# Four steps of a two-block network kernel resume a fixed time after their chain of small operations

## The chip, the cores and the metric

The kernel runs on one core of one Trainium2 chip. The metric is device time in microseconds (us) of one execution; lower is better. Of the core's engines, PE (TensorE) does the matrix products, DVE (VectorE) and ACT (ScalarE) work on tiles in SBUF and PSUM, POOL (GpSimd) does small vector work, and SP (SyncE) issues nearly all the transfers. Each engine takes its own instructions in the order in which the program wrote them, and waits at an instruction whose operands another engine has not finished.

## The reference

An activation x of 256 tokens by 1024 features goes through two blocks of two layers each, all in 32-bit floats.

```python
def rms_norm(x, g):
    y = x * rsqrt(mean(x * x, axis=-1) + EPS)
    return y * g

# block 1, each layer
x = x + 0.5 * swiglu(rms_norm(x, norm_ffn1[l]), w_gate, w_up, w_down)       # 1024 -> 2816 -> 1024
x = x + hybrid_mixer(rms_norm(x, norm_mix[l]), w_in[l], ..., w_out[l])      # two kinds of attention
x = x + 0.5 * swiglu(rms_norm(x, norm_ffn2[l]), ...)
# block 2, each layer
p = rmsnorm(x, norm1_g[l]) @ w_in[l]
y_rw  = rwkv7_branch(...)       # a recurrence over the tokens, 8 heads of 64
y_ret = retention_branch(...)
y_sg  = sgu_branch(...)
x = x + sum(gates * einsum('bsgc,gcd->bsgd', [y_rw, y_ret, y_sg], w_branch)) @ w_out[l]
x = x + conv_ffn(rmsnorm(x, norm2_g[l]), ...)
```

Two parts of the recurrence's branch matter here. Its keys are divided by their norms, `kk = kk / max(sqrt(sum(kk*kk)), 1e-12)`, and its result goes through a norm over each head, `(y - mean) * rsqrt(var + RW_GN_EPS) * lnx_g + lnx_b`, plus a bonus, times a gate.

## The kernel before

Tokens are two tiles of 128 (t = 0, 1). The weights, some 340 MB, stream once from memory. Each weight tile of 512 KB (`raw`) is split by ACT into a rounded part `wh` and by DVE into the remainder `wl`; the activations are split in the same way (`xh`, `xl`), and a product is three matmuls (`wh` by `xh`, `wh` by `xl`, `wl` by `xh`). In the profile `cf` and `pj` are PSUM tiles of projections into a layer, `acc` those of projections out of it.

What sets the order is a planner. While the Python code writes the program, the class `Meter` keeps an estimated clock for each engine. The large products are written by plain loops, which call `tick()` after every few matmuls. All the rest (norms, softmax, recurrence, splits of results) is written as generators, held as `Task`s with a rank. A generator that yields stops there, and `step()` says when it may go on: a bare `yield` makes it ready 0.1 us after the latest estimated end of what it has just issued; a list of tiles makes it ready 0.1 us after these; a function makes it wait for a condition. `tick()` runs each task that is ready by the estimated time of PE. So a task's next PE instruction is put behind those of the loop that were written in the meantime, and the real wait is what the estimate had too short. The planner's numbers act only while the program is written; on the chip there is only the order.

The four steps that the change touches:

- `norm()` with `wide` (every phase but block 1's mixers; eight phases, two tiles each): `mean_sq` squares the two halves of x on ACT, and POOL makes `xv` and the power `xr`. Then PE multiplies `xr` by the identity (the matmul `pt<-ident,xr`) to spread the factor along a row, and ACT copies it to `factor`. The projections run on x without the factor; DVE puts it in when it empties their PSUM tiles (`up<-cf,factor`, `up<-pj,factor`).
- `rw_keys()` (both layers of block 2): PE sums the squares of the keys (`pn`), DVE takes a maximum (`n`), POOL raises 128x16 numbers to the power -0.5, and PE spreads them (`pr<-ident,n`).
- `rw_products()`: for each tile and each of 8 heads PE makes masked products in `pM`, DVE copies them under a mask into `mrb` and `lm`, and PE multiplies `lm` by the values (`pX`, `pY`).
- `group_norm()`: four DVE operations on `Y`, then PE transposes it (`pt<-ident,Y`).

Of the kernel before, what the change touches and what calls it, by code (L numbers as in the profile page):

```python
# [222 lines left out]
class Builder:  # L223
# [48 lines left out]
    def step(self, task):  # L272
        self.meter.last = self.meter.t["PE"]
        try:
            y = next(task.gen)
        except StopIteration:
            self.tasks.remove(task)
            return
        if y is None:
            task.ready = self.meter.last + 0.1  # L280
        elif callable(y):
            task.cond = y
        else:
            task.ready = self.meter.of(y) + 0.1
# [246 lines left out]
    def norm(self, t, gi, wide=False, outer=None):  # L531


        nc = self.nc
        F = "p (k f) -> p k f"
        for i in range(2):
            yield from self.have(t, i)
            pt = self.ps("pt")
            for k in range(4):
                c = slice(k * P, (k + 1) * P)  # L540
                nc.tensor.transpose(pt[:, c], self.half(t, i)[:, c], self.ident)
            k = slice(i * 4, i * 4 + 4)
            g = self.gains if outer is None else self.both
            o = gi * KD if outer is None else 0
            g = g[:, o + i * 4:o + i * 4 + 4, None].to_broadcast([P, 4, P])
            xg = self.u("xg").rearrange(F, f=P)
            nc.vector.tensor_tensor(xg, pt.rearrange(F, f=P), g, ALU.mult)
            nc.scalar.copy(self.xh[:, k, t], xg)
            yield [self.xh[:, i * 4, t]]
            nc.vector.tensor_tensor(self.xl[:, k, t], xg, self.xh[:, k, t].bitcast(F32), ALU.subtract)  # L550
            self.ready_xT[t] = i + 1
        yield
        if outer is not None:
            ro = yield from self.row_norm(t, outer)
        r = yield from self.mean_sq(t)
        if outer is not None:
            nc.gpsimd.tensor_tensor(r, r, ro, ALU.mult)
        self.rstd[t] = r
        if wide:
            yield  # L560
            if not self.factor:
                self.factor.append(self.u("factor"))
            pt = self.ps("pt")
            nc.tensor.matmul(pt[:, :P], r.to_broadcast([P, P]), self.ident, start=True, stop=True)
            nc.scalar.copy(self.factor[0][:, t * P:(t + 1) * P], pt[:, :P])
            self.factored.append(t)
# [818 lines left out]
    def heads(self, ap):  # L1385
        return ap.rearrange("p (h d) -> p h d", d=64)

    def wide(self, ap, n=8):
        return ap[:, :, None].to_broadcast([P, n, 64])
# [78 lines left out]
    def rw_keys(self, l, st):  # L1468
# [16 lines left out]
        n = self.small("n2", 16, 2)  # L1485
        nc.vector.tensor_scalar_max(n, pn[:, :16], 1e-24)
        nc.gpsimd.tensor_tensor(n, n, self.mh, ALU.pow)
        yield
        for q in range(2):
            pr = self.ps("pr")  # L1490
            kk.append(self.pairs("kk"))
# [106 lines left out]
    def rw_products(self, l, st):  # L1598

        nc = self.nc  # L1600
        mm = nc.tensor.matmul
        yield lambda: "v" in st
        v = []
        for t in range(NT):
            v.append(self.tokens_on_partitions("vt", st["v"], t))
            yield
        st["vt"] = v
        yield lambda: "KT" in st and "queries" in st
        kr, BT, KT, mrb = (st[n] for n in ("kr", "BT", "KT", "m"))
        mk = self.c("mk3").bitcast(U32)  # L1610
        X, Y = [], []
        for t in range(NT):
            m = mrb[t]
            pX, pY = self.ps("pX", "pq"), self.ps("pY", "pq")
            for h in range(8):
                b, q, e = 64 * (h % 2), h // 4, h // 2 % 2
                pM = self.ps("pM")
                mm(pM[:, 0:P], BT[q][b:b + 64, e, t], kr[q][b:b + 64, e, t, 1], start=True, stop=True)
                mm(pM[:, P:3 * P], KT[q][b:b + 64, e, t], kr[q][b:b + 64, e, t].rearrange("p z f -> p (z f)"), start=True, stop=True)
                lm = st["lm"][h % 4]  # L1620
                nc.vector.copy_predicated(m[:, h], mk[:, 0:P], pM[:, 0:P])
                nc.vector.copy_predicated(lm, mk[:, P:3 * P], pM[:, P:3 * P])
                yield
                c = slice(h * 64, (h + 1) * 64)
                self.narrow(pX[:, c], lm[:, 0:P], v[t][:, c])
                self.narrow(pY[:, c], lm[:, P:2 * P], v[t][:, c])
            X.append(self.u("X"))
            Y.append(self.u("Y"))
            nc.scalar.copy(X[t], pX)
            nc.scalar.copy(Y[t], pY)  # L1630
            yield
        st.update(mrb=mrb, X=X, Y=Y)
# [94 lines left out]
    def group_norm(self, lnx, y, v, bonus, g, done):  # L1727
        nc = self.nc
        tt = nc.vector.tensor_tensor
        heads, wide = self.heads, self.wide  # L1730
        m = self.small("gm", 8)
        nc.vector.tensor_reduce(m, heads(y), AX.X, ALU.add)
        nc.vector.tensor_scalar(m, m, 1.0 / 64, None, ALU.mult)
        tt(heads(y), heads(y), wide(m), ALU.subtract)
        yield
        sq, bv = self.u("gsq"), self.u("gbv")
        nc.scalar.activation(sq, y, AF.Square)
        nc.gpsimd.tensor_tensor(heads(bv), heads(v), wide(bonus), ALU.mult)
        nc.gpsimd.tensor_tensor(bv, bv, lnx[1], ALU.add)
        yield [sq]  # L1740
        s2 = self.small("gs", 8)
        nc.vector.tensor_reduce(s2, heads(sq), AX.X, ALU.add)
        r = self.rstd_of(s2, 64, GN_EPS, 8)
        yield
        tt(heads(y), heads(y), wide(r), ALU.mult)
        tt(y, y, lnx[0], ALU.mult)
        tt(y, y, bv, ALU.add)
        tt(y, y, g, ALU.mult)
        yield
        yield from done(y)  # L1750


# [95 lines left out]
```

## Time and profile before

| what | before |
|---|---|
| median of 3 runs (lowest to highest) | 2075.59 us (2074.72 to 2077.48) |
| the profiled execution's own time | 2073.28 us |
| its span in the trace | 2071.3 us |
| PE busy | 2013.7 us (97%) |
| DVE, ACT, POOL busy | 1394.7, 1043.6, 149.8 us |
| mean rate of the transfers | 166 GB/s |

The span runs from the first to the last instruction of the program; the profiled execution took 2.0 us more than its span, and the median of the runs is 2.3 us above that execution. PE's clock as granted is shown in the profile as a share of full speed: 1.00 is 2.4 GHz and 0.50 is 1.2 GHz.

### The profile page before, as it was taken

Reading aid. Unit: us, or ns where it says so; the run is one execution under the profiler, and the core shown is the slowest. Engines: PE = TensorE matmul, PEld = TensorE weight load, DVE = VectorE, ACT = ScalarE, POOL = GpSimd, SP = SyncE. Lnnn points to the kernel's source line nnn. Section 1 sums busy time; section 2 is a strip of 40 time slices with the busy share of each in tenths; the row PEclk is TensorE's granted clock in tenths of the full one; section 3 lists DMA queues with packets and bytes.
Section 4 is the critical chain, followed back from the end, with each engine's and each line's share of the span. In section 5 each row is a group of like instructions: output and inputs, shape, how many; then the busy total and the mean of one; then the engine's idle time right before and its main releaser. Section 6 shows DMA issues by size and latency. Waiting matters only on the chain. (4 is left out here: it accounts for less than half of the span.)

```text
span 2071.3 us, 33930 instructions
## 1 busy us (share of the span) xinstructions
PE 2013.7 (97%) x13548; PEld 1776.8 (86%) x13548; DVE 1394.7 (67%) x2101; ACT 1043.6 (50%) x1605; POOL 149.8 (7%) x168
## 2 busy tenths in 40 slices
PE   8999999999999999999999999999999999999998
PEld 8998878998999887799887777889988877789997
DVE  6665666664666467666567957669955886667983
ACT  5444675443444366544455434456636444446652
POOL 0000000000000010000021031210001003110000
PEclk9999999999999999999999999999999999999999
DMA  9655623656655562356653434555664453465562
GB/s 315 195 181 152 213 83 113 198 177 194 218 180 185 157 214 92 122 174 193 186 175 114 147 112 136 180 162 177 191 200 134 133 153 98 153 192 176 177 194 97
DMA packets 246733, 343.98 MB, mean 166 GB/s; under 512 B 22064, under 2 KB 182192, under 8 KB 246448
## 3 DMA queue, kind: packets, MB, share of 16 engines
q1 hardware_dynamic: 244224, 340.20, 52.8%
q8 instruction: 106, 1.74, 0.4%
q10 hardware_dynamic: 2352, 1.63, 0.3%
q14 instruction: 51, 0.42, 0.1%
HBM read 339.68 MB, written 2.10 MB: 165 GB/s over the span
## 5 line engine op out<-in xcount | busy, mean ns | idle before, releaser
L191 DVE TENSOR_TENSOR wl<-raw,wh 128x1024 fp32r<-128x1024 f32 (+1 forms) x614 | 750.8, 1236 | 323.9 <-ACT wh L191 323.0
L191 ACT CAST wh<-raw 128x1024 fp32r<-128x1024 f32 (+1 forms) x614 | 639.3, 1046 | 585.9 <-PE cf L191 179.6
L191 PE MATMUL cf<-xh,wh 128*128 128x256 f32 x2112 | 524.7, 285 | 2.4 <-ACT wh L191 2.4
L191 PE MATMUL cf<-xl,wh 128*128 128x256 f32 x2112 | 523.0, 285 | 0.0
L191 PEld LDWEIGHTS cf<-xh,wh 128*128 128x128 f32 x2112 | 409.3, 194 | 3.0 <-ACT wh L191 2.8
L191 PEld LDWEIGHTS cf<-xl,wh 128*128 128x128 f32 x2112 | 409.2, 194 | 0.2
L191 PE MATMUL cf<-xh,wl 128*128 128x256 f32 x2112 | 300.3, 285 | 0.0
L191 PEld LDWEIGHTS cf<-xh,wl 128*128 128x128 f32 x2112 | 275.3, 194 | 0.0
L191 PE MATMUL pj<-wh,xh 128*128 128x512 f32 (+1 forms) x544 | 223.0, 410 | 4.5 <-DVE gate L191 2.0
L191 PE MATMUL pj<-wl,xh 128*128 128x512 f32 (+1 forms) x544 | 211.1, 388 | 0.0
L191 PE MATMUL pj<-wh,xl 128*128 128x512 f32 (+1 forms) x544 | 210.4, 387 | 0.0
L191 PE MATMUL acc<-wh,h 128*128 128x512 f32 x528 | 207.0, 392 | 0.0
L191 PE MATMUL acc<-wh,hl 128*128 128x512 f32 x528 | 205.6, 389 | 0.0
L191 PE MATMUL acc<-wl,h 128*128 128x512 f32 x528 | 205.5, 389 | 0.0
L191 PEld LDWEIGHTS pj<-wh,xh 128*128 128x128 f32 x544 | 102.8, 189 | 36.7 <-issue 9.9
L191 DVE TENSOR_TENSOR up<-cf,factor 128x512 f32<-128x512 f32 x132 | 90.6, 688 | 56.3 <-PE cf L191 56.2
L191 PEld LDWEIGHTS pj<-wh,xl 128*128 128x128 f32 x544 | 102.8, 189 | 21.4
L191 PEld LDWEIGHTS pj<-wl,xh 128*128 128x128 f32 x544 | 103.1, 189 | 16.9 <-DVE wl L191 0.9
L191 PEld LDWEIGHTS acc<-wh,hl 128*128 128x128 f32 x528 | 99.1, 188 | 20.9
L191 PEld LDWEIGHTS acc<-wh,h 128*128 128x128 f32 x528 | 99.2, 188 | 20.0
L191 PEld LDWEIGHTS acc<-wl,h 128*128 128x128 f32 x528 | 99.2, 188 | 19.9
L191 POOL TENSOR_SCALAR xv<-ss 128x1 f32<-128x1 f32 x24 | 20.2, 840 | 1142.6 <-ACT junk L191 1142.6
(314 smaller groups left out, 2489.6 us busy)
## 6 DMA issues: line engine op xcount, KB each, us to landing
raw<-w_in SPq DMA_DIRECT2D x156, 512.0 KB, 4.3
raw<-w_ffn_gate SPq DMA_DIRECT2D x88, 512.0 KB, 4.4
raw<-w_ffn_up SPq DMA_DIRECT2D x88, 512.0 KB, 4.8
raw<-w_ffn_down SPq DMA_DIRECT2D x88, 512.0 KB, 4.2
raw<-ffn_w_up SPq DMA_DIRECT2D x88, 512.0 KB, 4.7
raw<-ffn_w_down SPq DMA_DIRECT2D x44, 512.0 KB, 4.5
raw<-w_out SPq DMA_DIRECT2D x32, 512.0 KB, 3.7
raw<-w_branch SPq DMA_DIRECT2D x24, 512.0 KB, 4.5
```

Of the source, the lines that this page charges most:

```text
L191: return f(*args, **kw)
```

## The change

A generator may now yield a number: `step()` then makes it ready that many microseconds (of the planner's clock) after the latest estimated end, where a bare `yield` said 0.1. Four yields get such a number.

```diff
@@ step()
         if y is None:
             task.ready = self.meter.last + 0.1
+        elif isinstance(y, float):
+            task.ready = self.meter.last + y
         elif callable(y):
             task.cond = y
@@ norm()
         self.rstd[t] = r
         if wide:
-            yield
+            yield 5.0
@@ rw_keys()
         nc.gpsimd.tensor_tensor(n, n, self.mh, ALU.pow)
-        yield
+        yield 3.0
@@ rw_products()
                 nc.vector.copy_predicated(lm, mk[:, P:3 * P], pM[:, P:3 * P])
-                yield
+                yield 0.8
@@ group_norm()
         tt(y, y, g, ALU.mult)
-        yield
+        yield 2.0
         yield from done(y)
```

No instruction is added or taken away by this; the order on each engine changes, since the later steps are written later. Three places show how.

The first is ACT at the start of the second layer of block 1. `junk` are the squares of x, whose two tiles are `x_74` and `x_75`. One piece of the difference, with rows of the later splits left out:

```order
 L191 ACTIVATE junk,ss<-x_74 128x512 x2
 L191 CAST xh<-xg 128x4x128
-L191 CAST wh<-raw 128x1024 x2
-L191 COPY factor<-pt 128x128
-L191 CAST wh<-raw 128x1024
-L191 ACTIVATE junk,ss<-x_75 128x512 x2
...
+L191 CAST wh<-raw 128x1024 x3
+L191 ACTIVATE junk,ss<-x_75 128x512 x2
+L191 CAST wh<-raw 128x1024 x2
+L191 COPY factor<-pt 128x128
+L191 CAST wh<-raw 128x1024
+L191 COPY factor<-pt 128x128
```

Both copies of `factor` stand later, and the squares of the second tile no longer stand behind the first copy. On PE the matmul `pt<-ident,xr` of the first tile stands 48 matmuls of 256 columns later in four of the eight phases, and 44, 44, 45 and 54 later in the others; that of the second tile follows 25 to 85 matmuls behind it.

The second is PE in `rw_keys()` of block 2's first layer. Before:

```order
L191 MATMUL pn<-cst,sq 128x2 x8
L191 MATMUL pj<-xh,wh 128x256
L191 MATMUL pj<-xl,wh 128x256
L191 MATMUL pj<-xh,wl 128x256
L191 MATMUL pr<-ident,n_11382 64x128 x8
```

After, with the twelve further `pj` matmuls of the same three kinds left out:

```order
L191 MATMUL pn<-cst,sq 128x2 x8
L191 MATMUL pz<-waup,wag 128x512
L191 MATMUL pa<-wag,waup 128x256 x2
L191 MATMUL pj<-xh,wh 128x256
L191 MATMUL pj<-xl,wh 128x256
L191 MATMUL pj<-xh,wl 128x256
...
L191 MATMUL pr<-ident,n_11379 64x128 x8
```

Fifteen `pj`, one `pz` and two `pa` now stand where three `pj` stood. In the second layer it was three `pj` and one `pg`, and is now 24 `pj` and eight `pl`.

The third is PE around `group_norm()` of the first tile in block 2's first layer; `pS` are the steps of the recurrence's substitution, which read `X` or `sa`. Before:

```order
L191 MATMUL pS<-sa,Lo 32x64 x8
L191 MATMUL pj_12708<-wh,xh 128x512
L191 MATMUL pj_12708<-wl,xh 128x512
L191 MATMUL pj_12708<-wh,xl 128x512
L191 MATMUL pt<-ident,Y 128x128 x4
L191 MATMUL pj_12707<-wh,xh 128x512
L191 MATMUL pj_12707<-wl,xh 128x512
L191 MATMUL pj_12707<-wh,xl 128x512
L191 MATMUL pS<-X,dbd 32x64 x8
```

After, six `pj` stand in a row (the middle ones left out), and the transposes come behind the next substitution step:

```order
L191 MATMUL pS<-sa,Lo 32x64 x8
L191 MATMUL pj_12880<-wh,yTh 128x512
...
L191 MATMUL pj_12879<-wh,yTl 128x512
L191 MATMUL pS<-X,dbd 32x64 x8
L191 MATMUL pt<-ident,Y 128x128 x4
```

On DVE the two operations that make the next `X` stand right behind the four on `Y`, before and after, in the first layer. In the second layer one that empties a `gate` has come between them; DVE there, before:

```order
L191 TENSOR_TENSOR Y<-Y,rstd 128x512
L191 TENSOR_TENSOR Y<-Y,row_lnx_g 128x512
L191 TENSOR_TENSOR Y<-Y,gbv 128x512
L191 TENSOR_TENSOR Y<-Y,g 128x512
L191 TENSOR_TENSOR X<-pS,X 32x256 x2
```

After:

```order
L191 TENSOR_TENSOR Y<-Y,rstd 128x512
L191 TENSOR_TENSOR Y<-Y,row_lnx_g 128x512
L191 TENSOR_TENSOR Y<-Y,gbv 128x512
L191 TENSOR_TENSOR Y<-Y,g 128x512
L191 TENSOR_TENSOR gate<-pj_17697,gate 128x512
L191 TENSOR_TENSOR X<-pS,X 32x256 x2
```

So the four operations on `Y` are still ahead of `X`, which the substitution step before the transposes now reads on PE.

## Rows read from the trace of the kernel before

**Rows 1.** The page, busy time of PE: us (share of the span), instructions.
```profile
PE 2013.7 (97%) x13548; PEld 1776.8 (86%) x13548; DVE 1394.7 (67%) x2101; ACT 1043.6 (50%) x1605; POOL 149.8 (7%) x168
```

**Rows 2.** What PE waited for, whole span: us in total, times, longest us.
```profile
PE pt L191 <- POOL xr L191: 19.1, 9, 3.2
PE pr L191 <- POOL n L191: 4.9, 2, 2.8
...
PE pX L191 <- DVE lm L191: 3.6, 7, 1.3
PE pt L191 <- DVE Y L191: 3.4, 2, 1.7
...
PE pj L191 <- DVE gate L191: 2.0, 2, 1.0
```

**Rows 3.** PE in order of time from 345 us: start, us, [idle before <-releaser].
```profile
345.98 0.64 PE L191 MATMUL pt<-ident,xr 128*128 128x128 f32 x2 [3.24 <-POOL xr L191]
...
346.63 0.41 PE L191 MATMUL cf<-xl,wh 128*128 128x256 f32 x1
346.85 0.41 PE L191 MATMUL cf<-xh,wh 128*128 128x256 f32 x1
...
349.85 0.28 PE L191 MATMUL cf<-xl,wh 128*128 128x256 f32 x1
349.97 0.28 PE L191 MATMUL cf<-xh,wh 128*128 128x256 f32 x1
```

**Rows 4.** POOL in order of time, the same place.
```profile
342.62 1.84 POOL L191 TENSOR_SCALAR xv<-ss 128x1 f32<-128x1 f32 x1 [116.20 <-ACT junk L191]
344.54 1.39 POOL L191 TENSOR_TENSOR xr<-xv,mh 128x1 f32<-128x1 f32 x1
```

**Rows 5.** What ACT waited for in the first 60 us.
```profile
ACT wh L191 <- DMA raw<-w_ffn_up: 7.8, 4, 2.6
```

**Rows 6.** Stretches: us; PE, PEld, DVE, ACT, POOL busy (x); PE clock; DMA share; GB/s.
```profile
346.20:349.50 3.30, 3.30 (x17) 3.30 (x17) 0.44 (x1) 2.54 (x6) 0.86 (x2) 0.50 0.99 337
...
1374.90:1380.40 5.50, 5.50 (x26) 5.50 (x27) 1.85 (x2) 2.54 (x6) 2.66 (x4) 0.50 0.86 295
...
1092.80:1097.10 4.30, 4.30 (x27) 3.92 (x27) 1.66 (x4) 1.02 (x4) 0.20 (x1) 0.50 0.00 0
1182.50:1185.80 3.30, 3.30 (x10) 2.52 (x9) 3.27 (x4) 1.38 (x3) 1.46 (x1) 0.50 0.71 186
1602.30:1605.70 3.40, 3.40 (x25) 3.01 (x23) 0.67 (x2) 0.00 (x0) 0.00 (x0) 0.50 0.00 0
...
1880.60:1887.00 6.40, 6.40 (x54) 6.40 (x55) 1.98 (x3) 3.65 (x8) 0.87 (x2) 1.00 0.88 285
```

**Rows 7.** The key norms: POOL's power in the first layer; `pl` and `pg` on PE.
```profile
1089.75 2.91 POOL L191 TENSOR_TENSOR n<-n,mh 128x16 f32<-128x16 f32 x1 [15.98 <-DVE n L191]
...
1086.36 1.06 PE L191 MATMUL pl<-cst,sig 128*128 128x129 f32 x8
...
1597.40 1.10 PE L191 MATMUL pg<-gup,wag 128*128 128x512 f32 x2
```

**Rows 8.** The first layer's `group_norm`, first tile, on PE and DVE in order of time.
```profile
1255.48 0.63 PE L191 MATMUL pt<-ident,Y 128*128 128x128 f32 x4 [1.72 <-DVE Y L191]
...
1254.64 0.69 DVE L191 TENSOR_TENSOR Y<-Y,g 128x512 f32<-128x512 f32 x1
1255.36 0.88 DVE L191 TENSOR_TENSOR X<-pS,X 32x256 f32<-32x256 f32 x2
```

**Rows 9.** The same layer: last split of the recurrence's result (DVE), first matmuls that read it.
```profile
1277.79 0.69 DVE L191 TENSOR_TENSOR yTl<-pt,yTh 128x512 fp32r<-128x512 f32 x1
...
1330.77 0.39 PE L191 MATMUL pj<-wh,yTh 128*128 128x512 f32 x1
1331.00 0.39 PE L191 MATMUL pj<-wl,yTh 128*128 128x512 f32 x1
```

**Rows 10.** DVE, first emptying of a `pj` in block 2's second layer.
```profile
1575.92 0.69 DVE L191 TENSOR_TENSOR up<-pj,factor 128x512 f32<-128x512 f32 x1 [0.81 <-ACT factor L191]
```

## Prediction

> **What bounds the kernel now.** I read the page first, then the list of what PE waited for, then the order of time around the longest of these waits, and last the granted clock there.
>
> The page shows PE busy for 2013.7 us [rows 1] of a span of 2071.3: the kernel is bound by PE, and all that can be had without fewer matmuls is 57.6 us of idle time, and what PE loses while it is busy. The list of waits says who ends the idle time: `xr` from POOL 19.1 us in nine waits, `n` from POOL 4.9 in two, `lm` from DVE 3.6 in seven, `Y` from DVE 3.4 in two [rows 2]. Together 31.0 us, and each stands at one of the four yields that are changed.
>
> The order of time shows more than the idle time. At 345.98 the factor's matmul starts after 3.24 us of nothing, and after it the matmuls of 256 columns start 0.22 us apart; three us later they start 0.12 us apart [rows 3]. The windows say why: from 346.2 to 349.5 the granted clock is 0.50, the lower level of 1.2 GHz, while PE is busy throughout [rows 6]. So this wait costs its idle time and then half of a stretch of slow work, which the busy share hides.
>
> **The change, part by part.** No instruction is added or removed; the sum is over waits that go, stay or arise.
>
> *The factor, `yield 5.0`.* The chain behind the wait is two POOL operations, 1.84 and 1.39 us [rows 4]. After the change 44 to 54 more matmuls of 256 columns stand ahead of the factor's matmul, at 0.12 us each [rows 3] at least 5.3 us, against a longest wait of 3.2 [rows 2]. Nothing ahead of that chain on ACT gets longer (the squares of the second tile even lose the copy ahead of them). So these waits go whole. I take 1 us off, since one of the nine lies in the first 60 us, where ACT waits 7.8 us for weights [rows 5] and PE would reach that limit sooner: **18.1 us**. What becomes later is the emptying of the first accumulators. In the gated phases their banks are wanted four groups (384 matmuls, 46 us) on, so that is hidden. In block 2's mixers `mixed()` has four banks and its fifth group wants the first; in the first layer 39 matmuls, 4.7 us, stand between the second factor matmul and that group, and the emptying takes 0.69 us once the factor is there [rows 10]. It is covered by some 4 us; without that cover it would be a wait of about 1 us a layer.
>
> *The clock behind the factor.* Five of the nine waits are followed by a stretch at 0.50: four of 3.3 us like the one above, and one of 5.5 from 1374.9 [rows 6]. Half of each is lost: 4 x 1.65 + 2.75 = **9.4 us**. A sixth wait of 3.2 us, which ends at 1880.58, is followed by 1.00 throughout [rows 6], so a wait does not always cost this. With no wait, PE works without a break there before and after, and I take the whole. Bounds: 0 and 9.4.
>
> The Trainium skill ("TensorE: Matmul & The Clock Gate", Part 1) says that the slow clock is the default and activity releases it, and puts the penalty of a throttled stretch at its length times the share of the clock that is missing. By that the five stretches cost 18.7 x 0.5 = 9.35 us, the same as the rows.
>
> *The keys' norms, `yield 3.0`.* POOL's power takes 2.91 us [rows 7], and PE waits 2.8 us for it in one layer and 2.1 in the other [rows 2]. In the first layer twelve more `pj` come between, 12 x 0.12 = 1.4 us, and a `pz` with two `pa` that I count at nothing; so at most 1.4 us of the 2.8 remain. In the second, 21 more `pj` (2.5 us) and eight `pl`, of which four take 1.06 [rows 7], replace one `pg` of 1.10: 2.5 + 2.1 - 1.1 = 3.5, more than the 2.1. Saved: 1.4 + 2.1 = **3.5 us**, bounds 2.1 and 4.9. Both waits are followed by half clock, 4.3 us from 1092.8 and 3.4 from 1602.3 [rows 6], that is 2.15 and 1.7 lost. I take all of the second and half of the first, where a wait stays: **2.8 us**, bounds 0 and 3.9.
>
> *The masked products, `yield 0.8`.* 0.7 us more for each head is about three `pj` of 512 columns, 0.23 us each [rows 9]. The seven waits are 3.6 us with a longest of 1.3 [rows 2], so 0.7 does not clear the longest; there DVE is behind with other work. I take half, 1.8, and half of the half-clock stretch at 1182.5 [rows 6], 0.8: **2.6 us**, bounds 0 and 5.3.
>
> *The recurrence's result, `yield 2.0`.* Here the order speaks against a gain. In the trace PE reaches the transposes of `Y` at 1255.48 - 1.72 = 1253.76 and waits until DVE is through with `Y` at 1255.33; DVE begins the next `X` at 1255.36 and ends it at 1256.24 [rows 8]. After the change PE has three more `pj` (0.7 us) and comes at 1254.45 to the substitution step, which reads this `X`; and `X` is still queued behind the four operations on `Y`. It waits until 1256.24: 1.8 us in place of 1.7. In the second layer a `gate` operation on 512 columns, 0.69 us like that of [rows 10], has slipped ahead of `X`: 2.5 in place of 1.7. The wait for `Y` goes and one for `X` comes: **-0.9 us**, bounds -3 and +3.4.
>
> The Trainium skill ("TensorE: Matmul & The Clock Gate", Architectural detail) says that ACT and DVE are strict first-in first-out queues, while PE may pull weight loads ahead. By that rule `X` cannot pass `Y`, and this yield brings nothing; the trace agrees, with `X` starting 0.03 us after the last `Y`. If DVE could take `X` first, the sum would be 4.3 us larger.
>
> *What is shuffled by the way.* Block 2's mixers are rewritten in detail: the transfers of the inverse stand one or two weight loads earlier or later on SP, and POOL makes the keys' power ahead of two small products in the second layer. Waits of the kind that arises there are 2.0 us for `gate` [rows 2]; I allow as much anew: **-2.0 us**, bounds -5 and +2.
>
> Sum: 18.1 + 9.4 + 3.5 + 2.8 + 2.6 - 0.9 - 2.0 = 33.5 us. The span becomes 2037.8, the execution 2039.8, and the median, 2.3 above as before, **2042**.
>
> **The rivals.**
>
> *A: the idle time goes, the clock does not come back.* The half-clock stretches would lie where they lie for another reason, or fall anew on the waits that stay. For it: a wait of 3.2 us without a slow stretch [rows 6], and a stretch at 1182.5 behind a wait of only 1.3. Against it: five of six long factor waits have theirs right behind. Gain 18.1 + 3.5 + 1.8 - 0.9 - 2.0 = 20.5: 2055. The Trainium skill (the same page, Part 1) says that the watching is free-running, so that the same idle time may cost or not by where it falls, and this rival is what that would make of the waits that stay.
>
> *B: the mixers give back what they gain.* The four terms of block 2's mixers come out, with the shuffle, at -8 instead of 3.5 + 2.8 + 2.6 - 0.9 - 2.0 = +6.0 (each layer waits a few us more for `X`, `lm` and `gate`), and the gain is the factor's 27.5 less 8: 19.5, so 2056.
>
> *C: all goes.* Every wait of the four kinds and its slow stretch vanish: 31.0 + 9.4 + 3.9 + 1.7 = 46: 2030.
>
> *D: slower.* Each delay lengthens the one long chain of block 2: keys' norms, products, recurrence, result. The last split of that result ends at 1278.48 and the first matmul that reads it starts at 1330.77 [rows 9], 52.3 us of cover by gates and the other branches. The delays add at most 2.9 + 16 x 0.7 + 1.9 = 16.0 us in a layer, and in the order the last transposes stand 30 `pj` later, 6.8 us. Only when the chain is late by more than 52 us would PE stop; to be slower than before it must be late by some 70 us in both layers (52 + half of the 33.5). Against it stands a factor of four.
>
> *E: no change.* The planner's delay would have to be eaten by the planner itself, the matmul staying at its place; the order shows it moved.
>
> **How the numbers follow.** My forecast has 0.60, A 0.14, B 0.11, C 0.10, E 0.03, D 0.02. The predicted time is 2042. The range reaches to A, B and C: 2029 to 2058; the forecast's own range, with one wait or stretch more or less in each term, is 2035 to 2049. No change means within 0.2%, 4 us, about what a measurement of this kernel can tell: faster 0.95, within 0.03, slower 0.02.
>
> **What would show it right or wrong.** In the list of PE's waits `xr` should be gone or under 1 us; `n` at most 1.4; `Y` gone, and a new entry for `X` of some 4 us before `pS`; `lm` about half. The granted clock should be 1.00 behind the starts of the gated phases. PE's busy time should fall by some 13 us (9.4 + 2.8 + 0.8), though it executes the same matmuls, and its idle time by some 20. The number is wrong if the factor's matmuls still wait (then the real chain is longer than 5.3 us), if stretches of half clock are as many as before (A), or if the list for block 2's mixers grew (B).

## The result and the profile after

| what | before | after |
|---|---|---|
| median of 4 runs each (lowest to highest) | 2076.53 us (2074.72 to 2077.69) | 2048.27 us (2046.42 to 2049.43) |
| span in the trace | 2071.3 us | 2044.6 us |
| PE busy | 2013.7 us | 2004.7 us |
| PE idle (span less busy) | 57.6 us | 39.9 us |

The ratio after to before is 0.9864, with a 95% interval of 0.9847 to 0.9881: the kernel is 1.4% faster, by 28 us. The forecast was 2042 in a range of 2029 to 2058. In the span it is 26.7 us, 17.7 of idle time and 9.0 of busy time, where the forecast had about 20 and 13. Executions of one and the same kernel differ in their granted clock: of those of the kernel before, beside the experiments, the shortest took 2069.35 us at a mean clock of 0.993 and the longest 2081.67 us at 0.986. So a stretch of half clock that stands in one trace need not stand in the next execution.

The page of after, PE's row as in [rows 1]; the number of matmuls is the same:

```profile
PE 2004.7 (98%) x13548; PEld 1768.5 (86%) x13548; DVE 1390.2 (68%) x2101; ACT 1042.4 (51%) x1605; POOL 152.4 (7%) x168
```

What PE waited for in the whole span of after, the view of [rows 2] (us in total, times, longest us):

```profile
PE pt L191 <- DVE yret L191: 5.6, 1, 5.6
PE cf L191 <- ACT wh L191: 4.4, 2, 2.4
...
PE pj L191 <- DVE gate L191: 2.4, 2, 2.3
PE pj L191 <- DVE up L191: 1.9, 2, 1.2
PE pj L191 <- DVE xl L191: 1.9, 3, 0.7
PE pj L191 <- ACT xh L191: 1.5, 2, 1.0
...
PE pj L191 <- ACT sv L191: 1.3, 2, 0.9
...
PE pS L191 <- DVE X L191: 0.8, 2, 0.6
PE pX L191 <- DVE lm L191: 0.7, 2, 0.5
...
PE pr L191 <- POOL n L191: 0.4, 1, 0.4
```

All four entries of [rows 2] that the change aimed at are gone or under 1 us: `xr` from 19.1 to nothing, `n` from 4.9 to 0.4, `lm` from 3.6 to 0.7, `Y` from 3.4 to nothing. New at the head of the list is one wait of 5.6 us for `yret`, and several small ones have grown.

The place of [rows 3] and [rows 4], first POOL and then PE, in order of time (start, us, [idle before <-releaser]):

```profile
345.47 1.84 POOL L191 TENSOR_SCALAR xv<-ss 128x1 f32<-128x1 f32 x1 [116.25 <-ACT junk L191]
347.39 1.40 POOL L191 TENSOR_TENSOR xr<-xv,mh 128x1 f32<-128x1 f32 x1
349.38 0.30 POOL L191 TENSOR_SCALAR xv<-ss 128x1 f32<-128x1 f32 x1 [0.59 <-ACT junk L191]
349.76 0.56 POOL L191 TENSOR_TENSOR xr<-xv,mh 128x1 f32<-128x1 f32 x1
```

```profile
351.20 0.38 PE L191 MATMUL pt<-ident,xr 128*128 128x128 f32 x2
...
351.54 0.28 PE L191 MATMUL cf<-xl,wh 128*128 128x256 f32 x1
351.66 0.29 PE L191 MATMUL cf<-xh,wh 128*128 128x256 f32 x1
```

POOL is as slow as before, and is done with the first tile's `xr` at 348.79. The factor's matmul comes at 351.20, with 2.4 us to spare, and the `cf` matmuls behind it start 0.12 us apart.

Stretches of after with the clock, the columns of [rows 6]. The first two are starts of phases where before had 0.50 behind the wait for the factor ([rows 6] shows the first of them; the other three such places are at 1.00 in after too). The others are the stretches of half clock that after has outside of its first and last microseconds:

```profile
345.00:350.00 5.00, 5.00 (x44) 5.00 (x43) 4.50 (x5) 4.85 (x10) 3.77 (x4) 1.00 0.95 302
540.00:546.00 6.00, 6.00 (x53) 6.00 (x52) 3.82 (x4) 2.92 (x6) 0.00 (x0) 1.00 0.99 322
1685.00:1695.20 10.20, 6.15 (x28) 4.60 (x29) 2.91 (x8) 0.59 (x1) 3.22 (x5) 0.50 0.21 70
1118.40:1121.70 3.30, 3.30 (x9) 2.55 (x9) 2.87 (x10) 0.22 (x1) 0.00 (x0) 0.50 0.54 159
1746.50:1749.80 3.30, 3.30 (x23) 2.20 (x22) 2.25 (x4) 0.00 (x0) 0.00 (x0) 0.50 0.00 0
29.60:32.90 3.30, 3.30 (x18) 3.30 (x17) 3.14 (x4) 2.83 (x3) 0.00 (x0) 0.50 0.96 285
```

Three of these slow stretches stand at new waits (that of 1118.4 has only one of 0.27 us ahead of it). The longest is that at the wait for `yret`, in block 2's second layer. PE, DVE and POOL there, in order of time:

```profile
1689.05 1.25 PE L191 MATMUL pt<-ident,yret 128*128 128x128 f32 x4 [5.63 <-DVE yret L191]
```

```profile
1688.64 1.13 DVE L191 SCALAR_TENSOR_TENSOR yret<-py,rstd,rg 128x128 f32<-128x128 f32 x4 [8.07 <-POOL rstd L191]
```

```profile
1685.04 1.26 POOL L191 TENSOR_TENSOR ws<-ws,cst 128x512 f32<-128x512 f32 x1 [29.08 <-DMA ws<-ws]
...
1687.31 0.20 POOL L191 TENSOR_SCALAR var<-rss 128x4 f32<-128x4 f32 x1
1687.59 1.02 POOL L191 TENSOR_TENSOR rstd<-var,mh 128x4 f32<-128x4 f32 x1
```

The row of ACT that ends `rss`, and SP's load of `ws`:

```profile
1678.48 0.22 ACT L191 ACTIVATION_READ_ACCUMULATOR yret<-py 128x1 f32 x1
```

```profile
1680.35 0.41 SPq L191 DMA_DIRECT2D ws<-ws  x1
```

`yret` is the retention branch's result; its norm needs `rss`, which ACT has ready at 1678.70. POOL gets to it at 1687.31, since at the head of its queue stands the gating branch's mask on `ws`, a weight whose load SP issues only at 1680.35. In the order of before both norms of the retention branch stand ahead of `ws` on POOL; the new planning times turned that round. The Trainium skill ("TensorE: Matmul & The Clock Gate", Architectural detail) counts GpSimd among the strict first-in first-out queues; the trace agrees, with a ready operation held for 8.6 us.

In the second layer's `group_norm`, the place in [rows 8]'s manner, DVE and then PE:

```profile
1744.63 0.69 DVE L191 TENSOR_TENSOR Y<-Y,g 128x512 f32<-128x512 f32 x1
1745.35 0.69 DVE L191 TENSOR_TENSOR gate<-pj,gate 128x512 f32<-128x512 f32 x1
1746.08 0.89 DVE L191 TENSOR_TENSOR X<-pS,X 32x256 f32<-32x256 f32 x2
```

```profile
1746.10 0.55 PE L191 MATMUL pj<-wh,yTh 128*128 128x512 f32 x1 [2.27 <-DVE gate L191]
```

In the first layer, where the forecast reckoned, the wait for `X` is short:

```profile
1244.95 0.88 DVE L191 TENSOR_TENSOR X<-pS,X 32x256 f32<-32x256 f32 x2
```

```profile
1244.43 0.39 PE L191 MATMUL pj<-wh,yTl 128*128 128x512 f32 x1
1245.43 0.30 PE L191 MATMUL pS<-X,dbd 128*32 128x64 f32 x2 [0.61 <-DVE X L191]
```

### The profile page after: what moved, and what is told of

Same layout as the page of the kernel before. It is cut to its first block, busy times and chain, and to the rows that moved or that the text cites. A ratio compares the mean times of both kernels' runs of the same rounds, so it can differ in the third digit from the quotient of the medians.

```text
span 2044.6 us, 33928 instructions
## 1 busy us (share of the span) xinstructions
PE 2004.7 (98%) x13548; PEld 1768.5 (86%) x13548; DVE 1390.2 (68%) x2101; ACT 1042.4 (51%) x1605; POOL 152.4 (7%) x168
## 4 chain that ended last, share of the span: by engine, by line
PE 88%; DVE 7%; ACT 2%; DMA 1%; issue 1%; POOL 1%; SPq 0%; DVEq 0%; POOLq 0%; ACTq 0%
PE cf L191 37%; PE acc L191 22%; PE pj L191 20%; PE pt L191 3%; DVE Tt L191 2%; DVE wl L191 2%; PE sc L191 1%; PE pv L191 1%; DVE T L191 1%; PE pS L191 1%; DMA raw<-w_ffn_up 1%; PE pM L191 1%; ACT pe L191 1%; ACT pts L191 0%; PE pL L191 0%
## 5 line engine op out<-in xcount | busy, mean ns | idle before, releaser
L191 PEld LDWEIGHTS pj<-wh,xh 128*128 128x128 f32 x544 | 102.9, 189 | 35.5 <-issue 9.5
```

Source lines behind the costliest of these rows:

```text
L191: return f(*args, **kw)
```

## The experiments

Each kernel ran beside the kernel before on the same chip (median there 2074.0 to 2074.3 us), and each ratio is to that. In the short diffs, "after" is the changed kernel.

### Which yield brings the gain

*The factor's yield alone.* From after:

```diff
-        yield 3.0
+        yield
-                yield 0.8
+                yield
-        yield 2.0
+        yield
```

> The changed kernel with the 5.0 in norm() alone; the other three yields are bare again. Theory (the factor's waits and the half-clock stretches behind them are one thing): all nine xr waits (19.1 us) and the five stretches (9.4 us) go, at the start a wait for weights of about 2 us with 1.7 us of half clock comes, and the waits for n, lm and Y (11.9 us together) stay: gain 19.1 + 9.4 - 3.7 = 24.8, about 2052. Rival (the stretches lie there for another reason): 19.1 - 2.0 = 17, about 2059. If the wait for yret of the changed kernel comes from the other three yields, it is not here; if from the factor's, it is here with 5.6 us.

Measured: 2057.89 us, ratio 0.9922 (0.9909 to 0.9935). No wait for `xr` is left and no half clock stands behind the start of a gated phase, so the yield did what was forecast. The time is near the rival's all the same, since its list of PE's waits has a new one of 5.2 us, with half clock behind it, and `lm` 7.0 us in place of 3.6:

```profile
PE pX L191 <- DVE lm L191: 7.0, 10, 1.3
PE pS L191 <- ACT sa L191: 5.7, 2, 5.2
```

It is the same cause as in after with another victim: POOL's mask on `ws` waits 10.22 us for its load, and clearing `sa`, a tile of the recurrence, stands behind it. A row of POOL:

```profile
1708.79 1.26 POOL L191 TENSOR_TENSOR ws<-ws,cst 128x512 f32<-128x512 f32 x1 [10.22 <-DMA ws<-ws]
```

*All but the factor's yield.* From after:

```diff
-            yield 5.0
+            yield
```

> The changed kernel with norm()'s yield bare again, the other three kept. Theory: n gives 4.5 + 3.9 us of clock, lm 2.9 + 1.7, Y less X 2.6, together 15.6; the wait for yret takes 5.6 + 3.1 back and that for gate 2.0: gain 4.9, about 2072, with the xr waits of 19 us and five stretches at half clock behind them as before. Rival (the three steps carry half of the whole gain of 28): about 2062.

Measured: 2072.12 us, ratio 0.9991 (0.9978 to 1.0003): the other three bring nothing in this setting. The parts do not add up to the whole: the factor's yield alone takes 0.78% off, the other three alone 0.09%, all four 1.36%. The list of this kernel has both kinds of wait, and the wait for `yret`, which the factor's yield alone did not have, comes with the other three:

```profile
PE pt L191 <- POOL xr L191: 19.5, 8, 3.6
PE pt L191 <- DVE yret L191: 6.6, 1, 6.6
```

### Is the slow clock made by the idle time

*Matmuls in the factor's wait.* From the kernel before, in `norm()`, in six of the eight phases; the product is overwritten at once by the factor's:

```diff
             pt = self.ps("pt")
+            if t == 0 and self.phase in (2, 3, 5, 7, 8, 9):
+                for _ in range(18):
+                    self.tc.nc.tensor.matmul(pt[:, :2 * P], self.xh[:, 0, 0],
+                                             self.xh[:, 0:2, 0], start=True, stop=True)
```

> The kernel before, with 18 more matmuls of 256 columns on xh, about 2.2 us, right in front of the first tile's factor matmul in six of the eight phases (those whose wait is 2.1 us or more), into the same PSUM tile, which the factor then overwrites. No result changes and every later instruction waits for the same things. Theory (PE's idle time is what brings the clock down): the waits for xr fall from 19.1 to about 6 us, busy time takes their place, and the five half-clock stretches behind them go: gain 9.4, about 2067. Rival (the stretches have another cause, at the phase's start): 2076.5, with the stretches where they are.

Measured: 2066.99 us, ratio 0.9968 (0.9955 to 0.998). The kernel does 108 matmuls more than before, and is 7 us faster. In PE's order of time the wait of 3.24 us of [rows 3] is now 2.3 us of work and a wait of 1.08, and the window behind it runs at full clock:

```profile
343.73 2.32 PE L567 MATMUL pt<-xh 128*128 128x256 f32 x18
347.12 0.49 PE L191 MATMUL pt<-ident,xr 128*128 128x128 f32 x2 [1.08 <-POOL xr L191]
```

```profile
347.20:350.50 3.30, 3.30 (x28) 3.30 (x29) 0.96 (x2) 2.43 (x6) 0.86 (x2) 1.00 0.95 303
```

The factor comes no earlier here, so nothing is gained but the clock. This tells the forecast's second term from rival A: the slow stretches were made by the idle time ahead of them.

*A shorter delay.* `yield 2.0` in place of 5.0 in `norm()`, on the version with `ws` loaded early (next part).

> The kernel with the early load of ws (2041.8), with 2.0 in norm() in place of 5.0. In the order the first tile's factor matmul then stands 14 to 27, mostly 20, matmuls of 256 columns later than with a bare yield, 2.4 us at 0.12 us each, against waits of 3.2. Theory: waits for xr of some 0.8 us in five or six phases, about 4.5 us in all, and no half clock behind them (waits of 1.1 us had none in e4_fill_wait): 2046. Rival 1 (any wait there brings the half clock back): 2055. Rival 2 (the delay also costs, by late emptying, and less is better): 2041 or less.

Measured: 2042.55 us, ratio 0.985 (0.9836 to 0.9865). Waits for `xr` are back, five with 3.6 us in all and a longest of 0.8, and no half clock behind them. Here the theory had the waits right and the time wrong: it is no higher than with 5.0. PE is idle for 37.8 us of the span, against 35.5 with 5.0, the wait of 1.5 us at 28 us (below) being gone from this trace, and busy for 2002.4 us, against 2004.0.

### Where the new waits come from

*`ws` loaded early.* From after; the tile is no longer shared, and its load is issued with the recurrence's first rows:

```diff
@@ rw_init()
         st["w0"] = self.row(l, "w0")
+        self.ws = self.small("ws", 512, 1)
+        nc.sync.dma_start(self.ws, A["ws"][l])
@@ gating
-        ws = self.u("ws")
-        nc.sync.dma_start(ws, A["ws"][l])
+        ws = self.ws
```

> The changed kernel with the load of the gating weights ws issued at the start of each mixer of block 2 (a tile of its own), not when gating() begins; the multiplication on POOL stays where it is. Theory (POOL stands at the multiplication of ws until its load has landed, with the retention's var and rstd queued behind it): the wait of PE for yret, 5.6 us, and the half clock behind it, about 3.1, go: 2048.3 - 8.7, about 2040. Rival (yret is late for another reason, DVE's or ACT's queue): the wait stays, 2048.

Measured: 2041.79 us, ratio 0.9846 (0.9832 to 0.986), 0.0018 or 3.7 us below after; the two intervals overlap, so the time alone does not show a gain here. The wait for `yret` is gone from the trace. On POOL the mask now runs at once, long before it is needed:

```profile
1657.96 2.04 POOL L191 TENSOR_TENSOR ws<-ws,cst 128x512 f32<-128x512 f32 x1
```

*The same in the kernel before*, to see whether this load was a cost there:

> The kernel before with the early load of ws alone. Theory (the load is a hazard only where the new order puts the multiplication of ws ahead of what PE waits for): no PE wait hangs on it before, so the time is that of the kernel before within its spread, 2074. Rival (the early load is a gain of its own, by 8 us): 2066.

Measured: 2075.14 us, ratio 1.0005 (0.9995 to 1.0014): no change. So the late load cost nothing in the old order. That the new order makes it a cost shows in time with the factor's yield alone: 0.9922 (0.9909 to 0.9935) with the late load and 0.988 (0.9867 to 0.9894) with the early one (last run below), 8.7 us, and the 24.6 us that it then gains are close to the 24.8 that the theory had for this yield.

*The constants later.* On the early-`ws` version, the load of the constants (`cst`, 1.1 MB) is held until 24 weight tiles are taken rather than 4:

```diff
-yield lambda: self.take_next >= 4
+yield lambda: self.take_next >= 24
```

> The kernel with the early load of ws (2041.8), with the 1.1 MB load of constants cst, which nothing needs in the first phase, issued after 24 weight tiles instead of 4. Theory (in the changed kernel this load is issued 6 us earlier than before, at 14.4, and the weights wait behind it): the wait of PE for wh at 28 us, 1.5 us here and 2.0 with half clock behind it in the changed kernel, goes: 2040. Rival (the weights are late there by themselves): 2042.

Measured: 2039.6 us, ratio 0.983 (0.9816 to 0.9843). ACT's weight cast in the first phase, in after and then here:

```profile
26.97 1.04 ACT L191 CAST wh<-raw 128x1024 fp32r<-128x1024 f32 x1 [4.62 <-DMA raw<-w_ffn_up]
```

```profile
25.19 1.05 ACT L191 CAST wh<-raw 128x1024 fp32r<-128x1024 f32 x1 [2.30 <-DMA raw<-w_ffn_up]
```

In after, the constants' load is issued at 14.43 us, in before at 20.77, ahead of the weights that PE then waits for. With it moved, PE's wait at 28 us is gone; it was 1.97 us with half clock behind it in after, and 1.51 us without half clock in the version that this run starts from. The gain over that version, 0.0016, lies within the intervals; the gone wait is what the trace shows.

### The three small yields, one by one

All on the version with `ws` early (2041.79 us, ratio 0.9846).

*`group_norm()` bare*, `yield 2.0` to `yield`:

> The kernel with the early load of ws (2041.8), with group_norm()'s yield bare again. Forecast's view (DVE takes X behind the four operations on Y in any case, so this yield brings nothing): two waits for Y of 1.7 us come back, the waits for X (0.8) and for gate (2.3 and 1.7 of half clock) go, 2041 to 2043. Rival (PE really gains the 3.4 us): 2045.

Measured: 2042.33 us, ratio 0.9849 (0.9834 to 0.9865). The waits for `Y` are back (4.4 us in four), those for `gate` and `X` (2.4 and 0.8) gone: an exchange. At the place where PE waits 2.27 us for `gate` in after, the order on DVE is the same here, and PE waits for `Y`:

```profile
1744.38 0.63 PE L191 MATMUL pt<-ident,Y 128*128 128x128 f32 x4 [1.63 <-DVE Y L191]
```

*`rw_products()` bare*, `yield 0.8` to `yield`:

> The kernel with the early load of ws (2041.8), with rw_products()'s yield bare again. Theory from the two traces: the lm waits go from 0.5 back to some 3.6 us in seven or more places, with one stretch of half clock (1.7): 2046.5. Rival (heads that come later only shift the waits to something else): 2042.

Measured: 2041.68 us, ratio 0.9847 (0.9832 to 0.9862). `lm` is back with 3.2 us in seven waits, and `gate` fell from 2.4 to 0.6. This yield brings nothing measurable here: the rival was right, the theory's 2046.5 was not.

*`rw_keys()` bare*, `yield 3.0` to `yield`:

> The kernel with the early load of ws (2041.8), with rw_keys()'s yield bare again. Theory: the n waits come back, 4.9 us less what the new order hides, with 3.9 us of half clock behind them: about 2050. Rival (half clock there has to do with the many small matmuls, not with the wait): 2046.

Measured: 2049.11 us, ratio 0.9879 (0.9861 to 0.9898), 7 us more. The waits for `n` are back (4.1 us in two, the longest 2.3), and half clock stands at both. In the second layer it begins behind the wait. In the first it begins with it: the wait runs from 1080.57, and the clock is 1.00 up to 1080.5 and 0.50 from 1080.6:

```profile
1082.38 1.98 PE L191 MATMUL pr<-ident,n 128*64 128x128 f32 x16 [1.81 <-POOL n L191]
```

```profile
1080.60:1087.30 6.70, 4.92 (x33) 4.37 (x35) 2.14 (x4) 3.60 (x5) 1.73 (x1) 0.50 0.27 78
```

So in this layer the idle time of that wait did not bring the clock down; the last section comes back to what stands ahead of it. The rival's 2046 lies within the interval too, so the time does not tell the two apart.

*Only the factor's and the keys' yields:*

> The early load of ws with the yields of norm() (5.0) and rw_keys() (3.0) only; those of rw_products() and group_norm() bare. Theory (these two bring nothing, singly neither did): about 2042, with waits for lm and Y of 7 us in place of those for gate, X and others. Rival (each covers for the other): 2047 or more.

Measured: 2038.76 us, ratio 0.9828 (0.9814 to 0.9841). *Only the factor's:*

> The early load of ws with the yield of norm() (5.0) only. Theory: 2057.9 of e1_factor_only less the 5.2 us in which ACT's copy of sa waits for POOL behind the multiplication of ws, and some 2 us of half clock behind it: about 2050, 8 more than with the keys' yield too. Rival (the wait of e1_factor_only had another cause): 2057.

Measured: 2049.64 us, ratio 0.988 (0.9867 to 0.9894). The intervals of these two do not touch: the keys' yield is worth 0.52% of 2074 us, 10.8 us. The other two on top of it bring nothing: with all four it was 0.9846, and the intervals overlap.

The version with two yields and the early `ws` beats both kernels: its interval ends at 0.9841, below the 0.9847 at which that of after begins. With the later constants as well it was not tried.

## Why the prediction was right, and which term was wrong

The time lies in the range, faster by the mechanism that was forecast, and near the upper end of the forecast's own range of 2035 to 2049. That it came so near is in part luck, since terms that were too small stand against one that was far too small a loss. Term by term, from the lists of waits and the stretches of half clock of before and after, one trace of each:

| term | forecast | measured |
|---|---|---|
| waits for the factor | 18.1 | 19.1 |
| clock behind them | 9.4 | 9.4 |
| keys' norms, waits and clock | 6.3 | 4.5 + 3.9 = 8.4 |
| masked products, waits and clock | 2.6 | 2.9 + 1.7 = 4.6 |
| recurrence's result, `Y` less `X` | -0.9 | 3.4 - 0.8 = 2.6 |
| the rest, "what is shuffled by the way" | -2.0 | -17.4 |
| sum, as span | 33.5 | 26.7 |

The last measured row is what remains of 26.7 when the others (44.1) are taken off. Most of it can be named. The wait for `yret` with its clock is 5.6 + 3.1 = 8.7 (half of the 6.15 busy us at 0.50); the start 2.0 + 1.7; `gate` 0.4 + 1.7; `xl`, `xh` and `wl` some 3.3 more than before, `sv` and `sa` some 2.0; one more slow stretch at 1118.4, 1.7 (behind narrow matmuls, see the last section). That is 21.5. Against it stand one slow stretch of before that is gone and small waits for `rg` and `KT`, together about 3; what is left is 0.9 us from the measured row.

*The factor, and its clock.* Right in size and in cause. The waits went whole, and filling them with work gave back the clock alone, so rival A falls for the factor. That one wait of 3.2 us had no slow stretch behind it [rows 6] shows only that it is not every wait. With `ws` loaded early, this yield alone gains 24.6 us.

*The keys' norms.* Right, and too small by 2.1: in the first layer I let 1.4 us and half of the slow stretch remain, because I counted the `pz` and two `pa` at nothing. The longest wait left is 0.4 us. The clock's share in the first layer is less sure than I took it: the wait there runs from 1089.92 to 1092.72, and the clock falls at 1090.3, 0.4 us into it, so the wait can have made no more than a part of this stretch. The yield is worth 10.8 us with the factor's (7 with all the others).

*The masked products.* The waits went more fully than I took (half). But the runs show that this is not a gain: without the yield, `gate` waits less by nearly as much. The term belonged with the shuffle. Nor is the clock's 1.7 shown to be this wait's: in the trace of before with `ws` early the same wait is there, and the clock behind it is 1.00, where [rows 6] has 0.50 at 1182.5:

```profile
1180.57 0.34 PE L191 MATMUL pX<-vt,lm 128*64 128x64 f32 x4 [1.34 <-DVE lm L191]
```

```profile
1182.50:1185.80 3.30, 3.30 (x17) 2.69 (x15) 3.27 (x5) 2.26 (x3) 1.46 (x1) 1.00 0.71 222
```

*The recurrence's result.* The step "three more `pj`, so PE comes at 1254.45" failed. PE came later against DVE than that: it was through with the `pj` some 0.6 us ahead of the first half of `X`, not 1.8 ahead of the whole. The queue was read rightly, `X` starts 0.04 us after the last `Y`, and so was the net worth: nothing, as the run without this yield has it. The forecast's sign that showed this, about 4 us of `X`, did not come; the cost came as `gate`, 2.27 us with slow clock behind it: PE, which no longer stops for `Y`, stops for an operation that stands behind the four on `Y` in DVE's queue. That `gate` stands ahead of `X` is not the reason, since the run without this yield has the same order on DVE and no such wait.

*What is shuffled by the way.* This is the term that was mis-sized: -2.0 with a bound of -5, and it was -17.4. I took it from the kind of wait that was there in before (`gate`, 2.0 us), and did not read POOL's and SP's order for what could newly stand at a queue's head. There the order showed it: `ws`, which waits for a transfer, came ahead of the retention's norm. Taking that one cause away removed the wait; in time it is 3.7 us with overlapping intervals here, and 8.7 us clear of them where the factor's yield stands alone. Its median of 2041.79 is the forecast's number only because the terms above are larger than forecast while the rest of the shuffle stays, and the kernel before beside it ran at 2074.0, not 2076.5. I had also counted no half clock for new waits, though each slow stretch of 3.4 us costs 1.7. Rival B is thus right in part: the four mixer terms with the shuffle came to 44.1 - 28.5 - 17.4 = -1.8 us, between the forecast's +6.0 and B's -8, or +1.9 when the 3.7 at block 1's start are left out. C had the waits right, since all four kinds went, and missed what came in their place; D and E fall.

## What to carry to other kernels

A wait of a few microseconds in an otherwise dense stretch of matmuls can cost its idle time and half of a slow stretch behind it (five of six long waits for the factor did); look at the granted clock there, and put any independent work into the wait. When a planner's times are changed, read the new order of the small queues for an operation that waits for a transfer and has got ahead of ready work: half of what the shuffle cost here (8.7 of 17.4 us) went there, and an earlier load took that wait away. Delay only the steps whose wait is longest: with the load early, two of these four yields brought all of the gain. And read a clock term from more than one trace.

## What was not expected of the hardware

*POOL's first operations after a long idle time are slow.* `xv` on 128x1 takes 1.84 us after 116 us of idle time and 0.30 right after; the power 1.40 and 0.56. The rows above show both. It is this first price that made the chain long. That the idle time is the reason was not tried; after 14.88 us of it, an operation on 128x4 (`var`, in before at 1707.15) took 0.20.

*Half clock came without a wait.* In the version with two yields the clock is low for 10.2 us in which PE is always busy. The window, and what stands ahead of it in PE's order of time:

```profile
1613.00:1624.00 11.00, 11.00 (x41) 7.07 (x40) 7.69 (x23) 2.89 (x4) 0.00 (x0) 0.53 0.17 49
```

```profile
1610.21 0.51 PE L191 MATMUL pb<-rwo,r 128*128 128x2 f32 x4
1611.06 1.50 PE L191 MATMUL pb<-rwo,r 128*128 128x2 f32 x12 [0.35 <-POOL r L191]
```

Ahead of it PE makes sixteen matmuls of 2 columns in 2.4 us, with one wait of 0.35. The busy share calls that busy. The half clock of after at 1118.4 has the same matmuls ahead of it. In the run with `group_norm()` bare, the sixteen matmuls `pn` of 2 columns that the keys' norm starts with stand ahead of a slow stretch with no wait at all, PE being busy for all of 1070.0 to 1081.4:

```profile
1076.06 1.85 PE L191 MATMUL pn<-cst,sq 128*128 128x2 f32 x16
```

```profile
1078.10:1081.40 3.30, 3.30 (x14) 2.47 (x13) 2.44 (x5) 1.59 (x3) 3.08 (x1) 0.50 0.00 0
```

The same `pn` stand ahead of the keys' first wait in before and with that yield bare, where the clock fell within 0.4 us of the wait's beginning. In after they are passed at 1.00 (1072 to 1082). So half clock without a wait is shown; that the narrow matmuls are the cause was not tried, and they do not bring it each time.
